# Attention scores with 128-row products, key parts copied to the far halves by DMA, and both masks behind the products

## The chip, the cores and the metric

The program runs on one NeuronCore of a Trainium2 chip. Its engines are named as the profile names them: PE (TensorE, matrix products; PEld is its loading of weights), DVE (VectorE), ACT (ScalarE), POOL (GpSimd) and SP (SyncE). POOL and SP do no arithmetic here, they issue DMAs. The metric is the device time of one execution in microseconds (us).

## What is computed

Two layers over 512 positions of width 2048. Each layer normalises and modulates x, projects it, runs an S5 branch and a differential attention branch, and projects both back. Only the attention's scores are touched in their arithmetic:

```python
def diff_attention(q, k, v, lam, sub_g, lambda_init):
    ...
        sc = jnp.einsum('bqhmd,bkhmd->bhmqk', q_blk, k,
                        preferred_element_type=jnp.float32) * scale
        q_pos = i * Q_BLOCK + jnp.arange(Q_BLOCK)
        mask = key_pos[None, :] <= q_pos[:, None]
        sc = jnp.where(mask, sc, -jnp.inf)
        p = jax.nn.softmax(sc, axis=-1)
        w = p[:, :, 0] - lam * p[:, :, 1]
        return jnp.einsum('bhqk,bkhe->bqhe', w, vf)
```

There are 8 heads of two maps (m = 0, 1), each map with 64 dimensions, and 4 blocks of 128 queries. So scores are made in 2 x 8 x 4 = 64 blocks; block i sees N = 128 (i + 1) keys.

## The kernel before

Every large product is split for accuracy. An operand is held as a high part (rounded to float32r) and a low part (the rest), and one product becomes three: high by high, high by low, low by high (`mm3`). Weights come from memory in units of 128 x 1024 numbers, are split by ACT (`hi`) and DVE (`lo`), and each unit feeds one step of PE work, 24 products of 512 columns in most stages.

The order of instructions is written out in program order by `step`, which emits, between the PE work of one unit and the next, what the generators in `bg` (attention of a head, S5, modulation) have ready. Attention of head h is `attn_gen`. In its round t it emits `scores(t)`, `softmax(t - 1)`, `turn(t - 2)`, `values(t - 3)`, one round for each step. Heads follow each other every six steps, and PE meanwhile goes on with the q, k and gate projections of the next head, or with the GLU.

The two maps lie in the 128 partitions, map 0 in rows 0 to 63 and map 1 in rows 64 to 127. For a map m the tile `qk` holds `qa` (own half: high part of q, far half: low part of q) and `kb` (high part of k in both halves). So one 128-row product of `qa` and `kb` gives high by high plus low by high. The third term, high by low, comes from a product over the 64 rows of the own half of `qa` and of `KL`, the low part of k. Then a bf16 product of the identity and the triangle `maskb` adds the mask. All three write one PSUM bank (`bk5` for map 0, `bk6` for map 1). `qk_split` makes these parts for q (kind 1) and k (kind 0) in a later step than the projection.

Further pieces: `s5_prep` makes the S5 tables, once ahead of each layer, from `are`, `aim` and the step size; `mix` of the S5 output multiplies a tile by a 0/1 pattern `CS_TAP`; at the start the constants `cst` and parameters `par` are loaded ahead of x, and 80 bf16 products (`WARM`) run while x and the first weights arrive. In the first layer's modulation stage, `first_cols` starts a bank with a bf16 product of the identity by a column of zeros spread over 512 columns.

Of the kernel before, what the change touches and what calls it, by code (L numbers as in the profile page):

```python
# [10 lines left out]
F32 = mybir.dt.float32  # L11
F32R = mybir.dt.float32r
BF16 = mybir.dt.bfloat16
I32 = mybir.dt.int32
AF = mybir.ActivationFunctionType
# [6 lines left out]
P = 128  # L22
KT = D // P
NG = 64
# [7 lines left out]
PP_BG = PP_BA + DEPTH * 32  # L32
PP_SG = PP_BG + DEPTH * 16
PP_C = PP_SG + DEPTH
PP_ARE = PP_C + 16
PP_AIM = PP_ARE + DEPTH * NG
PP_W = PP_AIM + DEPTH * NG


CS_ID = 0  # L40
CS_MASK = CS_ID + P
CS_INVF = CS_MASK + P
CS_SG1 = CS_INVF + 1
CS_SG2 = CS_SG1 + 1
CS_SGR = CS_SG2 + 1
CS_TAP = CS_SGR + 1
CS_W = CS_TAP + P


# [3 lines left out]
NR = 2  # L53
NH = 4
SHARED = 8192
SIDE = 2560
WARM = 80


def idle(n):  # L60

    for _ in range(3 * n):
        yield


class Prog:
    def __init__(self, ctx, tc, io):
# [11 lines left out]
        self.lo = [sp.tile([P, 1024], F32R, name=f"lo{i}") for i in range(NH)]  # L79
        self.TOT = 52992 - 2 * KT * S - 2 * NH * 1024 - SHARED - SIDE  # L80
        self.sb = sp.tile([P, self.TOT], F32, name="sb")
# [27 lines left out]
    def v(self, off, n):  # L109
        return self.sb[:, off:off + n]  # L110
# [5 lines left out]
    def side(self, dt, name):  # L116

        self.sd = self.sp.tile([P, SIDE], dt, name=name, tag="side")

    def v2(self, off, n):  # L120
        return self.sd[:, off:off + n]
# [215 lines left out]
def build(ctx, tc, io):  # L337
    q = Prog(ctx, tc, io)
    nc = q.nc
    M, A, SUB = ALU.mult, ALU.add, ALU.subtract  # L340
    v = q.v
# [1 line left out]
    hth, htl = q.hth, q.htl  # L343


    cst = q.alloc(CS_W)
    par = q.alloc(PP_W)
    q.ident = v(cst + CS_ID, P)
    idm = v(q.alloc(128), 128).bitcast(BF16)
    idb, maskb = idm[:, 0:P], idm[:, P:]  # L350
    ones = v(q.alloc(P), P)
    zero = v(q.alloc(2), 2).bitcast(BF16)
    cos_o, sin_o = q.alloc(512), q.alloc(512)
# [12 lines left out]
    v2 = q.v2  # L366

    def pc(col, n=1):
        return v(par + col, n)

    def cc(col, n=1):
        return v(cst + col, n)
# [15 lines left out]
                wt0=(1, 384), wt1=(1, 512), of=(1, 512), sw=(1, 512), sm=(2, 32))  # L388
    ra.p, ra.wt = [ra.p0, ra.p1], [ra.wt0, ra.wt1]

    qa_o, kb_o, kl_o = [0, 512], [1024, 1536], 2048

    s5 = layout(R5, 4416, U=(2, 512), BE=(2, 384), K=(2, 128), D=(2, 128), PR=(1, 512),
                PI=(1, 512), GR=(1, 512), GI=(1, 512), A8=(1, 64))
# [16 lines left out]
    ada_o = [RA, RA + 1024]  # L411


    nc.sync.dma_start(out=v(cst, CS_W), in_=io["cst"])
    nc.sync.dma_start(out=v(par, PP_W), in_=io["par"])
    xt = [q.shared(4 * D, F32, "x0")]
    q.side(F32, "sd0")

    def xv(st, c0=0, n=D):
        return xt[0][:, st * D + c0:st * D + c0 + n]  # L420
# [4 lines left out]
    nc.vector.memset(ones, 1.0)  # L425
    nc.vector.memset(zero, 0.0)
    nc.vector.tensor_copy(out=idb, in_=cc(CS_ID, P))
    nc.vector.tensor_copy(out=maskb, in_=cc(CS_MASK, P))  # L428


    t16 = v(small_o, 16)
# [4 lines left out]
    def setup_gen():  # L436
# [9 lines left out]
        nc.vector.tensor_copy(out=tw[0], in_=posi)  # L446
        q.ts(tw[0], tw[0], cc(CS_INVF), M)
        yield from idle(1)
# [182 lines left out]

    def s5_prep(l):
        T = [v(x, 64) for x in s5.tab]
        are, aim = pc(PP_ARE + NG * l, NG), pc(PP_AIM + NG * l, NG)
        lst, step, xr, th, er, co, si = T[0:7]
        q.dma(lst, io["lstep"][l].partition_broadcast(P))
        yield from idle(3)
        yield from q.exp_acc(step, lst, T[7:10], 64)
        yield from idle(1)
        q.tt(xr, are, step, M)  # L640
        q.tt(th, aim, step, M)
        yield from q.exp_acc(er, xr, T[7:10], 64)
        yield from idle(2)
        yield from q.sincos(co, si, th, T[7:12])
        yield from idle(2)
        PR, PI, GR, GI, TW = (tab3(x) for x in (s5.PR, s5.PI, s5.GR, s5.GI, s5.tw))
        a1r, a1i, nr, den, fr, fi, t0 = T[12:19]
        q.tt(a1r, er, co, M)
        q.tt(a1i, er, si, M)
        q.ts(nr, a1r, 1.0, SUB)  # L650
        q.tt(den, are, are, M)
        q.tt(t0, aim, aim, M)
        q.tt(den, den, t0, A)
        nc.vector.reciprocal(out=den, in_=den)
        yield from idle(1)
        q.tt(fr, nr, are, M)
        q.tt(t0, a1i, aim, M)
        q.tt(fr, fr, t0, A)
        q.tt(fr, fr, den, M)
        q.tt(fi, a1i, are, M)  # L660
        q.tt(t0, nr, aim, M)
        q.tt(fi, fi, t0, SUB)
        q.tt(fi, fi, den, M)
        yield from idle(1)
        nc.vector.tensor_copy(out=PR[:, :, 0], in_=a1r)
        nc.vector.tensor_copy(out=PI[:, :, 0], in_=a1i)
        for n in (1, 2, 4):
            ar = PR[:, :, n - 1].unsqueeze(2).to_broadcast([P, NG, n])
            ai = PI[:, :, n - 1].unsqueeze(2).to_broadcast([P, NG, n])
            yield from q.cmul(PR[:, :, n:2 * n], PI[:, :, n:2 * n], ar, ai, PR[:, :, 0:n], PI[:, :, 0:n], TW[:, :, 0:n])  # L670
            yield from idle(1)
        nc.vector.tensor_copy(out=GR[:, :, 0], in_=fr)
        nc.vector.tensor_copy(out=GI[:, :, 0], in_=fi)
        frb = fr.unsqueeze(2).to_broadcast([P, NG, 7])
        fib = fi.unsqueeze(2).to_broadcast([P, NG, 7])
        yield from q.cmul(GR[:, :, 1:8], GI[:, :, 1:8], frb, fib, PR[:, :, 0:7], PI[:, :, 0:7], TW[:, :, 0:7])
        q.ts(v(s5.GI, 512), v(s5.GI, 512), cc(CS_SG2), M)

        q.ts(v(s5.A8, 64), PI[:, :, 7], cc(CS_SG2), M)
        yield from idle(1)  # L680
# [82 lines left out]
    def s5_state_gen(l):  # L763
# [107 lines left out]
        for j in range(8):  # L871
            if j < 7:
                s5_load_be(l, j + 1, 128)
                load_m(j + 1)
                s5_load_u(l, j + 1)
            be = v(s5.BE[j % 2], 384).rearrange("p (f g q) -> p f g q", f=3, g=8)
            O = o.A[j % 2]
            On4 = O.rearrange("p (g s e) -> p g s e", g=8, s=8)
            T4 = o.T.rearrange("p (g s e) -> p g s e", g=8, s=8)
            pr = PR[:, 8 * j:8 * j + 8, :].unsqueeze(3).to_broadcast([P, 8, 8, 16])  # L880
            pi = PI[:, 8 * j:8 * j + 8, :].unsqueeze(3).to_broadcast([P, 8, 8, 16])
            q.tt(On4, pr, be[:, 1].unsqueeze(2).to_broadcast([P, 8, 8, 16]), M)
            q.tt(T4, pi, be[:, 2].unsqueeze(2).to_broadcast([P, 8, 8, 16]), M)
            q.tt(O, O, o.T, SUB)
            Mb = o.B[j % 2].rearrange("p (g f) -> p g f", g=8)
            q.tt(Mb, Mb, cc(CS_TAP, P).unsqueeze(1).to_broadcast([P, 8, P]), M)
            yield
            if j > 0:
                gelu(j - 1)
            yield  # L890
            b = bank[3 - j % 2]
            U = v(s5.U[j % 2], 512)
            for g in range(8):
                q.mm(b[:, g * 64:(g + 1) * 64], Mb[:, g], U[:, g * 64:(g + 1) * 64], True, False)
                q.mm(b[:, g * 64:(g + 1) * 64], O[:, g * P:(g + 1) * P], X[:, 8 * j + g, 0:64], False, True)
            yield
# [8 lines left out]
    def attn_gen(l, h):  # L905
        n = h % 2
        V, Z = v(ra.v, 512), v(ra.za[n], 512)
        KL = v2(kl_o, 512)
        OF = v(ra.of, 512)
        sm = ra.sm[n]  # L910
        ssum, ssq = v(sm, 8), v(sm + 8, 4)
# [6 lines left out]
        def scores(i):  # L918
            N = (i + 1) * P
            assert S5[l].r == 8  # L920
            for m in range(2):
                qa, r = v2(qa_o[m] + i * P, P), slice(64 * m, 64 * m + 64)
                q.mm(q.sc[m][:, 0:N], qa, v2(kb_o[m], N), True, False)
                q.mm(q.sc[m][:, 0:N], qa[r], KL[r, 0:N], False, False)
                q.mm(q.sc[m][:, i * P:N], idb, maskb, False, True)

        def softmax(i):
# [234 lines left out]
    def layer(l):  # L1162
# [131 lines left out]
        def qk_split(kind):  # L1294
            x = v(ra.x[kind], 512)
            for m in range(2):
                r, far = slice(64 * m, 64 * m + 64), slice(64 - 64 * m, 128 - 64 * m)
                if kind == 0:
                    kb = v2(kb_o[m], 512)
                    q.act(kb[r], x[r], AF.Copy)  # L1300
                    q.act(kb[far], x[r], AF.Copy)
                    q.tt(v2(kl_o, 512)[r], x[r], kb[r].bitcast(F32), SUB)
                else:
                    qa = v2(qa_o[m], 512)
                    q.act(qa[r], x[r], AF.Copy)
                    q.tt(qa[far], x[r], qa[r].bitcast(F32), SUB)
# [259 lines left out]
def _layout(x, c, positions, norm_g, w_ada, b_ada, w_in, w_out, ssm_a_re, ssm_a_im, ssm_b_re, ssm_b_im,  # L1566
# [80 lines left out]
    par[:, PP_SG:PP_C] = pk(sub_g)  # L1647
    par[:, PP_C:PP_ARE] = pk(c)
    par[0:64, PP_ARE:PP_AIM] = ssm_a_re.reshape(-1, 64).T
    par[64:, PP_ARE:PP_AIM] = ssm_a_re.reshape(-1, 64).T  # L1650
    par[0:64, PP_AIM:PP_W] = ssm_a_im.reshape(-1, 64).T
# [4 lines left out]
    cst[:, CS_ID:CS_ID + P] = np.eye(P)  # L1656
    cst[:, CS_MASK:CS_MASK + P] = np.where(r[None, :] <= r[:, None], 0.0, NEG)
    invf = np.float32(10000.0) ** (-np.arange(32, dtype=f) / np.float32(32))
    cst[:, CS_INVF] = invf[r % 32]
    cst[:, CS_SG1] = np.where(r < 64, 1.0, -1.0)  # L1660
    cst[:, CS_SG2] = np.where(r < 64, -1.0, 1.0)
    cst[:, CS_TAP:] = (r[None, :] // 16 + r[:, None] % 8) >= 7
    cst[:, CS_SGR] = np.where(r % 64 < 32, -1.0, 1.0)
# [27 lines left out]
```

## Time and profile before

| | |
|---|---|
| device time, median of 3 runs | 1971.81 us (1969.84 to 1972.72) |
| the profiled execution | 1970.02 us, of which the span from the first to the last instruction is 1967.6 us |
| busy share of the span | PE 99%, PEld 84%, DVE 70%, ACT 41%, POOL 9% |
| the 16 attention heads | about 43 us each, at 441 to 780 us and at 1390 to 1730 us |

The profiled execution's own time is its span and 2.4 us around it, and it lies 1.8 us under the median. Matrix products are pipelined: a product's row in the trace overlaps the next one's, so what a product costs is read from the distance between the starts of two rows, not from the length of a row.

### The profile page before, as it was taken

To read this page: it belongs to the slowest core of one execution; us is meant where nothing else is said; L and a number is where in the kernel's file an instruction comes from. 1 tells how busy PE (TensorE), PEld (TensorE's weight loads), DVE (VectorE), ACT (ScalarE), POOL (GpSimd) and SP (SyncE) were. 2 spreads that over 40 slices of the span, in tenths; PEclk is the share of its full clock that TensorE was granted. 3 is DMA by queue.
4 is the path that set the end of the run, shared out by engine and by line. 5 is a ranking of instruction groups with operands and counts; after the bars stand their busy time and mean duration, and the time that the engine had idled before them with its cause. 6 is when DMAs were issued, how large, how long until landed. Compare 5 with 4: busy or idle time off the path is not lost.

```text
span 1967.6 us, 28067 instructions
## 1 busy us (share of the span) xinstructions
PE 1945.2 (99%) x10552; PEld 1655.1 (84%) x10560; DVE 1371.1 (70%) x2603; ACT 811.7 (41%) x1510; POOL 180.7 (9%) x280
## 2 busy tenths in 40 slices
PE   8999999999999999999999999999999999999998
PEld 7888898888777778888899899888777777888887
DVE  7867866987778787779867434797777776643444
ACT  6333234444444554322245234433444445532222
POOL 0003230220000000000001220032000000000000
PEclk9999999999999999999999999999999999999999
DMA  8976652666555845687544433376655584345323
GB/s 320 367 290 228 193 147 96 207 188 209 157 159 179 198 153 174 223 301 238 169 161 134 127 116 109 99 226 202 184 169 167 156 187 125 97 152 215 97 86 118
DMA packets 117864, 350.38 MB, mean 178 GB/s; under 512 B 31680, under 2 KB 32128, under 8 KB 115296
## 3 DMA queue, kind: packets, MB, share of 16 engines
q1 hardware_dynamic: 97632, 277.27, 44.2%
q0 software_dynamic: 20096, 71.32, 11.6%
q8 instruction: 82, 1.34, 0.3%
q14 instruction: 54, 0.44, 0.1%
HBM read 309.60 MB, written 30.54 MB: 173 GB/s over the span
## 4 chain that ended last, share of the span: by engine, by line
PE 93%; DMA 2%; DVE 2%; issue 1%; ACT 1%; SPq 0%; POOL 0%; ACTq 0%; DVEq 0%
PE bk L143 92%; PE bk L151 2%; DMA sb<-in_wada 2%; DVE lo L128 1%; DMA sb<-in_ssm_d 1%; DVE sb L137 1%; DVE sb L128 0%; DMA sb<-in_w 0%; DVE htl L128 0%; ACT hi L125 0%; ACT sd L125 0%; ACT x L125 0%; DVE sb L132 0%; SPq L424 0%; DVE x L128 0%
## 5 line engine op out<-in xcount | busy, mean ns | idle before, releaser
L128 DVE TENSOR_TENSOR lo<-sb,hi 128x1024 fp32r<-128x1024 f32 x288 | 351.5, 1222 | 404.7 <-ACT hi L125 382.7
L125 ACT ACTIVATE hi<-sb 128x1024 fp32r<-128x1024 f32 x288 | 304.4, 1059 | 624.2 <-PE bk L143 465.4
L143 PE MATMUL bk<-hth,hi 128*128 128x512 f32 x1280 | 512.9, 401 | 0.0
L143 PE MATMUL bk<-hth,lo 128*128 128x512 f32 x1280 | 499.6, 390 | 0.0
L143 PE MATMUL bk<-htl,hi 128*128 128x512 f32 x1280 | 498.8, 390 | 0.0
L143 PE MATMUL bk<-hi,hth 128*128 128x256 f32 (+1 forms) x1088 | 358.1, 329 | 1.7 <-ACT hth L125 1.3
L143 PE MATMUL bk<-hi,htl 128*128 128x256 f32 (+1 forms) x1088 | 355.8, 327 | 0.9 <-DVE htl L128 0.9
L143 PE MATMUL bk<-lo,hth 128*128 128x256 f32 (+1 forms) x1088 | 355.7, 327 | 0.5 <-DVE lo L128 0.5
L137 DVE SCALAR_TENSOR_TENSOR sb<-sb 128x512 f32<-128x512 f32 (+7 forms) x654 | 320.5, 499 | 20.3 <-DMA sb<-in_wada 1.5
L143 PEld LDWEIGHTS bk<-hth,lo 128*128 128x128 f32 x1280 | 240.3, 188 | 51.6
L143 PEld LDWEIGHTS bk<-htl,hi 128*128 128x128 f32 x1280 | 240.9, 188 | 48.1 <-issue 1.9
L143 PEld LDWEIGHTS bk<-hth,hi 128*128 128x128 f32 x1280 | 241.1, 188 | 47.6 <-issue 1.9
L128 DVE TENSOR_TENSOR sb<-sb 128x4 f32<-128x4 f32 (+7 forms) x461 | 220.2, 495 | 22.5 <-DMA sb<-in_ssm_d 8.9
L143 PEld LDWEIGHTS bk<-hi,hth 128*128 128x128 f32 x1088 | 207.0, 190 | 19.8 <-ACT hth L125 1.5
L143 PEld LDWEIGHTS bk<-hi,htl 128*128 128x128 f32 x1088 | 206.9, 190 | 19.0 <-DVE htl L128 1.4
L143 PEld LDWEIGHTS bk<-lo,hth 128*128 128x128 f32 x1088 | 207.0, 190 | 18.0 <-DVE lo L128 0.7
L143 PE MATMUL bk<-sb 128*128 128x128 f32 (+4 forms) x1112 | 165.0, 279 | 7.8 <-DVE sb L428 3.7
L143 PE MATMUL bk<-gt,hi 128*128 128x512 f32 x512 | 159.6, 393 | 0.0
L143 PEld LDWEIGHTS bk<-sb 128*128 128x128 f32 x904 | 118.5, 193 | 9.6 <-issue 3.8
L125 ACT ACTIVATE sb<-bk,sb 128x512 f32<-128x512 f32 (+3 forms) x144 | 77.1, 540 | 104.8 <-DVE sb L132 104.8
L125 ACT ACTIVATE sb<-bk 128x512 f32<-128x512 f32 (+3 forms) x212 | 87.2, 444 | 64.7 <-PE bk L143 34.9
L143 PEld LDWEIGHTS bk<-gt,hi 128*128 128x128 f32 x512 | 94.8, 188 | 18.8
(112 smaller groups left out, 1812.7 us busy)
## 6 DMA issues: line engine op xcount, KB each, us to landing
sb<-in_w SPq DMA_DIRECT2D x288, 512.0 KB, 4.0
sb<-in_wada SPq DMA_DIRECT2D x185, 512.0 KB, 4.7
sb<-uD POOLq DMA_DIRECT2D x32, 256.0 KB, 5.6
ss<-kD POOLq DMA_DIRECT2D x16, 512.0 KB, 6.0
sb<-sb SPq DMA_DIRECT2D x128, 64.0 KB, 3.9
sb<-in_be POOLq DMA_DIRECT2D x32, 192.0 KB, 4.4
x<-in_x SPq DMA_DIRECT2D x4, 1024.0 KB, 11.6
uD<-sd POOLq DMA_DIRECT2D x16, 256.0 KB, 3.2
```

The costliest lines, as they stand in the source:

```text
L125: self.nc.scalar.activation(out=out, in_=in_, func=func, **kw)
L128: self.nc.vector.tensor_tensor(out=out, in0=a, in1=b, op=op)
L137: self.nc.vector.scalar_tensor_tensor(out=out, in0=a, scalar=s, in1=b, op0=op0, op1=op1)
L143: return self.nc.tensor.matmul(out, lhsT=l, rhs=r, start=a, stop=z)
L151: return self.nc.tensor.transpose(out, in_, self.ident)
```

## The change

The product over 64 rows becomes one over 128 rows. For that the low part of k must stand in both halves, so each map gets its own `kl` next to its `kb` in the `qk` tile. `qk_split` computes own halves only (one ACT and one DVE operation for a map), and a DMA from the POOL queue copies `kb` and `kl` of the own half, 64 x 1024 numbers (256 KB), into the far half. The mask products of both maps follow the four score products.

The `qk` tile grows by 512 columns. Room for it is made elsewhere: `CS_MASK` and `CS_TAP` are loaded into the side tile and kept as bf16 only, and `are` and `aim` are no longer resident but are loaded by two POOL DMAs in `s5_prep`.

```diff
-    qa_o, kb_o, kl_o = [0, 512], [1024, 1536], 2048
+    qa_o, kb_o, kl_o = [0, 512], [1024, 2048], [1536, 2560]
...
-    nc.sync.dma_start(out=v(cst, CS_W), in_=io["cst"])
-    nc.sync.dma_start(out=v(par, PP_W), in_=io["par"])
...
+    nc.sync.dma_start(out=v(cst, CS_P), in_=io["cst"][:, 0:CS_P])
+    nc.sync.dma_start(out=v2(2560, 2 * P), in_=io["cst"][:, CS_P:CS_W])
+    nc.sync.dma_start(out=v(par, PP_P), in_=io["par"][:, 0:PP_P])
...
-    nc.vector.tensor_copy(out=maskb, in_=cc(CS_MASK, P))
+    nc.vector.tensor_copy(out=maskb, in_=v2(2560, P))
+    nc.vector.tensor_copy(out=tapb, in_=v2(2560 + P, P))
...
-        are, aim = pc(PP_ARE + NG * l, NG), pc(PP_AIM + NG * l, NG)
+        are, aim = T[19:21]
+        q.dma(are, io["par"][:, PP_ARE + NG * l:PP_ARE + NG * (l + 1)])
+        q.dma(aim, io["par"][:, PP_AIM + NG * l:PP_AIM + NG * (l + 1)])
...
-            q.tt(Mb, Mb, cc(CS_TAP, P).unsqueeze(1).to_broadcast([P, 8, P]), M)
+            q.tt(Mb, Mb, tapb.unsqueeze(1).to_broadcast([P, 8, P]), M)
...
             for m in range(2):
-                qa, r = v2(qa_o[m] + i * P, P), slice(64 * m, 64 * m + 64)
+                qa = v2(qa_o[m] + i * P, P)
                 q.mm(q.sc[m][:, 0:N], qa, v2(kb_o[m], N), True, False)
-                q.mm(q.sc[m][:, 0:N], qa[r], KL[r, 0:N], False, False)
+                q.mm(q.sc[m][:, 0:N], qa, v2(kl_o[m], N), False, False)
+            for m in range(2):
                 q.mm(q.sc[m][:, i * P:N], idb, maskb, False, True)
...
-                    kb = v2(kb_o[m], 512)
+                    kb, kl = v2(kb_o[m], 512), v2(kl_o[m], 512)
                     q.act(kb[r], x[r], AF.Copy)
-                    q.act(kb[far], x[r], AF.Copy)
-                    q.tt(v2(kl_o, 512)[r], x[r], kb[r].bitcast(F32), SUB)
+                    q.tt(kl[r], x[r], kb[r].bitcast(F32), SUB)
+                    both = v2(kb_o[m], 1024)
+                    q.dma(both[far], both[r])
```

On PE, the last score block of a head (i = 3, N = 512, here head 0 of layer 0) stands as follows, before and then after. `bk5_81` and `bk6_82` are the score banks of the two maps, `qk0` the tile of q and k parts, `sb_75` as an operand of the 128x128 products behind a LDWEIGHTS row is identity and mask, and the row ahead is the last product of a projection.

```order
L143 MATMUL bk1_77<-hth_65,lo1_72 128x512
L143 MATMUL bk5_81<-qk0_2990 128x512 x2
L143 LDWEIGHTS sb_75
L143 MATMUL bk5_81<-sb_75 128x128
L143 MATMUL bk6_82<-qk0_2990 128x512 x2
L143 LDWEIGHTS sb_75
L143 MATMUL bk6_82<-sb_75 128x128
L143 MATMUL bk2_78<-sb_75 128x128
```

```order
L145 MATMUL bk1_77<-hth_65,lo1_72 128x512
L145 MATMUL bk5_81<-qk0_2994 128x512 x2
L145 MATMUL bk6_82<-qk0_2994 128x512 x2
L145 LDWEIGHTS sb_75
L145 MATMUL bk5_81<-sb_75 128x128
L145 LDWEIGHTS sb_75
L145 MATMUL bk6_82<-sb_75 128x128
L145 MATMUL bk2_78<-sb_75 128x128
```

Each "x2" is the product with `kb` and the one with the low part of k; before, the second of them is the one over 64 rows, now both are over 128. The mask of map 0 moved from between the maps to behind them.

On the POOL queue the two copies of a head stand where that head's k is split. This is the place of head 0 of layer 0, before and after; `uD0`, `yD0` and `vD0` are tensors in memory (S5 input, S5 output, values), `ss0` the S5 tile.

```order
L140 DMA ss0_1217<-kD0_88 128x8x128
L140 DMA sb_75<-uD0_84 128x8x64
L140 DMA yD0_86<-sb_75 128x8x64 x2
L140 DMA sb_75<-vD0_90 128x4x128
L140 DMA yD0_86<-sb_75 128x8x64
```

```order
L142 DMA ss0_1221<-kD0_88 128x8x128
L142 DMA sb_75<-uD0_84 128x8x64
L142 DMA qk0_2994<-qk0_2994 64x1024 x2
L142 DMA yD0_86<-sb_75 128x8x64 x2
L142 DMA sb_75<-vD0_90 128x4x128
L142 DMA yD0_86<-sb_75 128x8x64
```

The copies stand ahead of the stores of the S5 output that DVE and ACT finish later; nothing else on this queue moved.

## Rows read from the trace of the kernel before

**Rows 1.** The page's chain that ended last: share of the span by engine.

```profile
PE 93%; DMA 2%; DVE 2%; issue 1%; ACT 1%; SPq 0%; POOL 0%; ACTq 0%; DVEq 0%
```

**Rows 2.** PE's waits, whole span, longest first: us in total, times, longest.

```profile
PE bk L143 <- DVE sb L428: 3.7, 1, 3.7
...
```

**Rows 3.** Busy time in windows over the 16 heads: sum and mean.

```profile
...
sum 675.00, PE 675.00 PEld 536.40 DVE 502.46 ACT 338.76 POOL 25.67; mean PE 42.19 PEld 33.53 DVE 31.40 ACT 21.17 POOL 1.60
```

**Rows 4.** PE timeline, score block N = 512: start us, us, engine, line, operation.

```profile
507.56 0.39 PE L143 MATMUL bk<-hth,lo 128*128 128x512 f32 x1
507.79 0.82 PE L143 MATMUL bk<-qk 128*128 128x512 f32 x2
...
508.11 0.50 PE L143 MATMUL bk<-qk 64*128 64x512 f32 x1
...
508.54 0.23 PE L143 MATMUL bk<-sb 128*128 128x128 bf16 x1
508.57 0.90 PE L143 MATMUL bk<-qk 128*128 128x512 f32 x2
509.41 0.51 PE L143 MATMUL bk<-sb 128*128 128x128 bf16 x3
```

**Rows 5.** Weight loads of the same block; in brackets the idle time before.

```profile
507.56 0.19 PEld L143 LDWEIGHTS bk<-qk 128*128 128x128 f32 x1
508.10 0.18 PEld L143 LDWEIGHTS bk<-qk 64*128 64x128 f32 x1 [0.35 <-issue]
508.53 0.10 PEld L143 LDWEIGHTS <-sb 128*128 128x128 bf16 x1 [0.24 <-issue]
```

**Rows 6.** PE timeline, blocks of 128, 256 and 384 keys of the same head.

```profile
486.33 0.83 PE L143 MATMUL bk<-sb 128*128 128x128 f32 x6
486.92 0.56 PE L143 MATMUL bk<-qk 128*128 128x128 f32 x2
...
487.94 0.23 PE L143 MATMUL bk<-sb 128*128 128x128 bf16 x1
...
493.53 0.59 PE L143 MATMUL bk<-qk 128*128 128x256 f32 x2
...
494.70 0.23 PE L143 MATMUL bk<-sb 128*128 128x128 bf16 x1
...
500.65 0.79 PE L143 MATMUL bk<-qk 128*128 128x384 f32 x2
...
502.13 0.23 PE L143 MATMUL bk<-sb 128*128 128x128 bf16 x1
```

**Rows 7.** PE timeline in the first modulation stage, around the zero product of `first_cols`.

```profile
57.06 0.40 PE L143 MATMUL bk<-hth,lo 128*128 128x512 f32 x1
57.52 0.61 PE L143 MATMUL bk<-sb 128*128 128x128 f32 x4
```

**Rows 8.** Weight load of that zero product.

```profile
57.29 0.10 PEld L143 LDWEIGHTS <-sb 128*128 128x128 bf16 x1 [0.27 <-issue]
```

**Rows 9.** Timelines, head 6 of layer 0: its k subtractions, its first scores.

```profile
689.33 1.38 DVE L128 TENSOR_TENSOR qk<-sb,qk 64x512 fp32r<-64x512 f32 x2
...
700.29 0.56 PE L143 MATMUL bk<-qk 128*128 128x128 f32 x2
```

**Rows 10.** DMA issues by line: KB each, median us to landing.

```profile
sb<-uD POOLq DMA_DIRECT2D x32, 256.0 KB, 5.6
```

**Rows 11.** Timeline of the start: parameter loads, and DVE's wait for x.

```profile
1.19 0.42 SPq L415 DMA_DIRECT2D sb<-in_par  x1
1.25 0.67 POOL L140 DMA_DIRECT2D sb<-in_lstep  x1 [0.81 <-POOLq L1679]
...
19.74 0.17 DVE L134 TENSOR_SCALAR sb<-sb 128x4 f32<-128x4 f32 x1 [2.32 <-ACT hth L125]
```

**Rows 12.** DVE groups by shape, 370 to 442 us (S5 output, layer 0): busy, mean ns.

```profile
L128 DVE TENSOR_TENSOR ss<-ss,sb 128x1024 f32<-128x1024 f32 x12 | 14.4, 1221 | 0.8 <-DMA ss<-kD 0.7
```

**Rows 13.** Busy time in 15 windows of 9 us of that stage, both layers.

```profile
...
sum 135.00, PE 135.00 PEld 120.48 DVE 111.84 ACT 51.16 POOL 40.66; mean PE 9.00 PEld 8.03 DVE 7.46 ACT 3.41 POOL 2.71
```

More of the change, by code (lines that the diff above doesn't have):

```diff
@@ L34 @@
 PP_C = PP_SG + DEPTH
-PP_ARE = PP_C + 16
+PP_P = PP_C + 16
+PP_ARE = PP_P
 PP_AIM = PP_ARE + DEPTH * NG
@@ L40 @@
 CS_ID = 0
-CS_MASK = CS_ID + P
-CS_INVF = CS_MASK + P
+CS_INVF = CS_ID + P
 CS_SG1 = CS_INVF + 1
@@ L45 @@
 CS_SGR = CS_SG2 + 1
-CS_TAP = CS_SGR + 1
+CS_P = CS_SGR + 1
+CS_MASK = CS_P
+CS_TAP = CS_MASK + P
 CS_W = CS_TAP + P
@@ L55 @@
 SHARED = 8192
-SIDE = 2560
+SIDE = 3072
 WARM = 80
@@ L343, in build @@
     hth, htl = q.hth, q.htl
-    cst = q.alloc(CS_W)
-    par = q.alloc(PP_W)
+    cst = q.alloc(CS_P)
+    par = q.alloc(PP_P)
     q.ident = v(cst + CS_ID, P)
-    idm = v(q.alloc(128), 128).bitcast(BF16)
-    idb, maskb = idm[:, 0:P], idm[:, P:]
+    idm = v(q.alloc(192), 192).bitcast(BF16)
+    idb, maskb, tapb = idm[:, 0:P], idm[:, P:2 * P], idm[:, 2 * P:]
+    idm = idm[:, 0:2 * P]
     ones = v(q.alloc(P), P)
@@ L907, in attn_gen @@
         V, Z = v(ra.v, 512), v(ra.za[n], 512)
-        KL = v2(kl_o, 512)
         OF = v(ra.of, 512)
```

## The prediction

> **What bounds the kernel now.** I read the chain of waits first: PE holds 93% of it [rows 1], so a change that shortens PE's work shortens the program wherever PE never waits. The view of waits shows how rarely it does: no wait of it adds up to more than 3.7 us in the whole span, and the longest is at the start [rows 2]. Then the stages. In the windows over the sixteen heads PE is busy for all of its 42.19 us a window, DVE for 31.40, ACT for 21.17 [rows 3]. So a microsecond that PE saves in a head is a microsecond of the program, until another engine fills the head. The heads also hold the only place where PE does something odd, and the timeline of PE and of its weight loads shows it.
>
> **What a score block costs before.** I measure from the start of its first product to the start of its second mask; what follows the second mask is the same before and after. With 512 keys: 507.79 to 509.41, 1.62 us [rows 4]. The products alone, at the distance of ordinary 512-column products (507.56 to 507.79, 0.227 us), would be 4 x 0.227 = 0.91. The rest is in the steps into and out of the 64-row product. The 128-row product at 507.79 is followed 0.32 us later by the 64-row one at 508.11, which is followed 0.43 us later by the mask at 508.54: 0.09 and 0.20 too much [rows 4]. The weight loads say why. A load for 128 rows starts with the product ahead of it (507.56, both views) and is hidden under it; the 64-row load starts at 508.10, with its own product, after PE's loading side stood idle 0.35 us, and the mask's load again waits, to 508.53, behind the 64-row product [rows 4, 5]. So PE runs empty on the way into 64 rows and on the way back. The other blocks cost 486.92 to 487.94 (1.02), 493.53 to 494.70 (1.17) and 500.65 to 502.13 (1.48) [rows 6].
>
> **What it costs afterwards.** Four 128-row products, of which the last is followed by a bf16 load, and one mask ahead of the second mask.
> - Products: 0.227 us for 512 columns [rows 4]. For 128 columns the distance of the 128-column products ahead of the smallest block: 0.111 (six of them take 0.83 us from 486.33, and the first score product at 486.92 stands 0.03 behind the start of the last) [rows 6]. Between these, 384 and 256 columns take at least their proportion of 512 (0.170 and 0.114) and at most the straight line from 0.111 to 0.227 (0.188 and 0.150).
> - The step from a 128-row product of the large kind to a bf16 product: the program before has it, in the first modulation stage. There a product at 57.06 is followed by an unrecorded bf16 product of 512 columns, whose load stands at 57.29, and the next product starts at 57.52: 0.46 us for two times 512 columns, 0.23 each [rows 7, 8]. The load does come late, but nothing is lost, so I put this step at 0. The other end is the 0.20 above.
> - First mask to second mask: no two bf16 products of 128 columns stand together in the trace. Below: 128 columns in proportion to 512, 0.057. Above: 0.111, the distance of 128-column products with full loads [rows 6]. I take 0.08.
> - Where short products precede the block, its first product is recorded 0.08 early (486.92 is those 0.03 behind the last of the six, not 0.111) and its distance to the next is longer by as much [rows 6]. That holds for the blocks of 128 and 384 keys, before and after, so 0.08 is added there.
>
> Blocks then cost 0.91 + 0.08 = 0.99 (512 keys), 0.08 + 0.44 + 0.08 = 0.60 (128), and at the lower distances 0.08 + 0.68 + 0.08 = 0.84 (384) and 0.46 + 0.08 = 0.54 (256). Saved: 0.63, 0.42, 0.64 and 0.63, together 2.32 us a head; at the upper distances the last two save 0.57 and 0.48, together 2.10. I take 2.25, nearer the proportion, since a product of 256 columns has twice the columns under which a load is hidden at 0.111. Times 16: **36.0 us**, bounds 33.6 and 37.1.
>
> **A rule against it.** The Trainium skill, "TensorE: Matmul & The Clock Gate", Part 3 on packing small matmuls, says that a weight load overlaps a running product only when the row groups differ. By that, four products on the same 128 rows would each pay their load, and the change would lose time; that is the fourth rival below. This case's trace disagrees: the load at 507.56 runs beside a product on the same rows [rows 4, 5]. Another page of the Trainium skill, "TensorEngine Tiling (Array Packing)", section "Tiling Modes", under key properties, says that changing the tiling mode drains the engine while changing the tile does not; by that rule nothing drains in the new block, which bears out the 0 above, and the trace agrees for the way into and out of 64 rows.
>
> **The rest of the change.**
> - ACT loses 32 copies of a half. ACT is busy half of a head [rows 3], so this is worth nothing by itself; it lets the subtractions come a little earlier.
> - POOL gains 32 copies of 256 KB. Cost nothing, hidden by the time between k's split and the first scores. The tightest head that I found is head 6: the second subtraction ends at 690.71, the first score product starts at 700.29, 9.6 us later [rows 9]. The nearest DMA in size on that queue lands in 5.6 us [rows 10]; with two issues of 0.67, as of another DMA on that queue [rows 11], that is 6.9, a margin of 2.7 us. Without that cover every head would wait. Queued behind the copies on POOL are the load of v, wanted three steps later, and in head 0 the stores of the S5 output, which wait for DVE until after the copies anyway.
> - The first product of each map in `scores(0)` now waits for a copy as well as for DVE. If the copy has landed this costs nothing.
> - The start: one more SP issue ahead of the loads of x, 0.42 us, and x and the weights behind it gate the first products: **+0.4 us**. On POOL the step size is issued two DMAs later, 2 x 0.67 = 1.3 us; DVE's table work ahead of the norm shifts with it, but DVE stood idle 2.32 us there [rows 11]. Bounds 0 to 1.7 us.
> - `mix`'s multiplication now reads bf16 in one operand: 16 operations of 1.22 us [rows 12]. I take no change; if the mixed operand doubled it, DVE has 9.00 - 7.46 = 1.5 us idle in the 9 us of each [rows 13]. Before layer 1, `are` and `aim` are loaded by two small DMAs with nothing waiting.
>
> **Sum.** 1970.0 (the profiled execution's own time) - 36.0 + 0.4 = 1934.4. It lies 1.8 us under the median of the runs shown, so as a median **1936 us**. Its own range: the product distances move it by -1.1 to +2.4 us, the mask's by up to 64 x 0.03 = 2 either way, the start by -0.4 to +1.3, the median by about 1.5: 1932 to 1941.
>
> **Rivals.**
> 1. *The bf16 load still empties PE.* Then 0.20 us of the old block stays in each of the 64: 12.8 us back, **1949**. For it: the masks' loads are late in the old block, and the zero product's load is late too [rows 5, 8]. Against: no time is lost around the zero product [rows 7].
> 2. *Another engine fills the head.* DVE would have to find its 31.4 us in 40.0; on average it does, but its work is uneven, and PE could begin to wait on `lo` or on the softmax. Half a microsecond to one a head gives back 8 to 16 us: **1944 to 1952**. Against: PE waits nowhere in the heads now [rows 3].
> 3. *The copies come late* (slower). If a copy takes 11 us instead of 5.6, the first scores wait 11 + 1.3 - 9.6 = 2.7 us in each head, 43 us in all: **1979**. Priced with the tightest head; it decides from about 10.5 us of landing on, where the wait eats 2.25 us a head. Against: the stage moves little data on POOL, and 5.6 us is the median of 32 like-sized DMAs [rows 10].
> 4. *Loads are not hidden on equal rows* (slower): 256 score products pay 0.19 each [rows 5], 49 us; less the 36 saved, **1985**. The trace speaks plainly against it.
> 5. *The 64 rows are not what costs*, but the second product into a bank; the 128-row product then pays the same: **1972**. Against: projections send 24 products into one bank at 0.227 us each.
>
> **How the numbers follow.** Chances: forecast 0.78, first rival 0.10, second 0.05, third 0.03, fourth 0.02, fifth 0.02. The forecast's own range leaves 0.22 outside, so I widen it over the first rival: 1932 to 1949. A measurement of this kernel can tell about 0.2% (4 us) from no change. Faster: forecast, first and second rival, 0.93; within 0.2%: the fifth, 0.02; slower: the third and fourth, 0.05.
>
> **What would show it.** Right: in the 512 block four products 0.23 us apart, no idle before their loads, the mask's load late but the first mask 0.23 to 0.24 us behind the fourth product, heads of about 40.9 us instead of 43, no PE wait for a DMA in the heads. Wrong: a distance of 0.4 us ahead of the first mask (first rival), PE waiting for `qk` copies (third) or for `lo` (second), or a first product later than 20 us into the span (start).

## The result: 1939.3 us instead of 1972.2

| | before | changed |
|---|---|---|
| device time, median of 4 runs | 1972.20 us (1969.84 to 1972.72) | 1939.32 us (1938.70 to 1940.49) |
| ratio | | 0.9836, 95% interval 0.9819 to 0.9853 |
| the profiled execution, its span | 1970.02 us, 1967.6 us | 1940.49 us, 1938.7 us |

The change wins 32.9 us between the medians and 29.5 between the two profiled executions. 1936 was forecast, with a range of 1932 to 1949.

**The block.** PE's timeline of the changed kernel, score block N = 512 of the head of [rows 4], in five narrow stretches, so that each product's start shows (a row ends with the last product that it counts):

```profile
504.24 0.62 PE L145 MATMUL bk<-qk 128*128 128x512 f32 x2
504.47 0.61 PE L145 MATMUL bk<-qk 128*128 128x512 f32 x2
504.70 0.61 PE L145 MATMUL bk<-qk 128*128 128x512 f32 x2
504.92 0.39 PE L145 MATMUL bk<-qk 128*128 128x512 f32 x1
505.15 0.28 PE L145 MATMUL bk<-sb 128*128 128x128 bf16 x2
```

The weight loads of the same block:

```profile
504.02 0.87 PEld L145 LDWEIGHTS bk<-qk 128*128 128x128 f32 x4
505.15 0.12 PEld L145 LDWEIGHTS <-sb 128*128 128x128 bf16 x2 [0.26 <-issue]
```

The four products start 0.22 to 0.23 us apart, the distance of the ordinary 512-column products in [rows 4]. Their loads begin at 504.02, one product ahead, with no idle between them. The mask's load is late, as foretold, and nothing is lost: the first mask starts 0.23 behind the fourth product. Before, 0.32 and 0.43 stood between these products [rows 4].

Blocks of 128 and 256 keys, the same head:

```profile
485.12 0.64 PE L145 MATMUL bk<-qk 128*128 128x128 f32 x4
485.60 0.28 PE L145 MATMUL bk<-sb 128*128 128x128 bf16 x2
...
491.26 0.63 PE L145 MATMUL bk<-qk 128*128 128x256 f32 x4
491.74 0.29 PE L145 MATMUL bk<-sb 128*128 128x128 bf16 x2
```

To the first mask it is 0.48 us in both. Counted from a block's first product to the product after its second mask, a typical block (the median of the 16 heads) went from 1.06 to 0.58 us (128 keys), 1.20 to 0.57 (256), 1.54 to 0.93 (384) and 1.69 to 1.03 (512). That saves 0.48, 0.63, 0.62 and 0.65 us, 2.39 us a head before rounding. The same saving is seen in whole heads. The next view has the first seven heads of layer 0, in windows that run from the first score block of one head to that of the next, before and then changed (the windows of [rows 3] are of other lengths, so their mean of 42.19 us is not the length of a head):

```profile
sum 301.61, PE 301.61 PEld 240.18 DVE 227.72 ACT 153.78 POOL 12.02; mean PE 43.09 PEld 34.31 DVE 32.53 ACT 21.97 POOL 1.72
```

```profile
sum 284.90, PE 284.90 PEld 238.20 DVE 227.62 ACT 144.82 POOL 19.75; mean PE 40.70 PEld 34.03 DVE 32.52 ACT 20.69 POOL 2.82
```

**What was given back.** 16 x 2.39 is 38.2 us, and the span became only 28.9 shorter. The chain that ended last has less PE than in [rows 1]. In the view of PE's waits the first two of the following lines stood before as well, with 3.7 us each at the most [rows 2]; the wait for q's split (`qk`) is new, and the one for ACT's `sb` had been 0.4 us:

```profile
PE 89%; DVE 4%; DMA 3%; issue 1%; ACT 1%; SPq 0%; POOL 0%; ACTq 0%; DVEq 0%
```

```profile
PE bk L145 <- DMA sb<-in_wada: 4.5, 1, 4.5
PE bk L145 <- DVE sb L433: 3.6, 1, 3.6
PE bk L145 <- DVE qk L130: 2.5, 1, 2.5
PE bk L145 <- ACT sb L127: 1.9, 5, 0.6
```

I compared the distance from each score block to the next in both traces. It is shorter by the same amounts everywhere but for four places. The start gives back 0.6 us (first score block at 442.3 instead of 441.7). Head 8, the first of layer 1 counted from 0, gives back 5.8 in the distances to and from its first block. Head 13 gives back 2.4, and the step to the last block of head 7 0.5. Together that is 9.3, and 38.2 less 9.3 is 28.9.

**Head 8.** The changed kernel's queues and DVE there, SP first, then POOL, then DVE:

```profile
1359.48 3.62 SPq L1354 DMA_DIRECT2D sb<-sb  x4
```

```profile
1359.91 0.54 POOL L142 DMA_DIRECT2D qk<-qk  x1 [3.41 <-DVE qk L130]
1360.63 0.52 POOL L142 DMA_DIRECT2D qk<-qk  x1 [0.18 <-issue]
1361.15 0.80 POOL L142 DMA_DIRECT2D sb<-vD  x1
```

```profile
1369.01 2.02 DVE L130 TENSOR_TENSOR sb<-sb 128x512 f32<-128x512 f32 x3 [8.67 <-DMA sb<-sb]
```

The four small DMAs at 1359.48 are `qk_out`'s swaps of q, which `rope` needs. The two copies of k, 512 KB, go out beside them, and DVE waits 8.67 us for the swaps. Before, that wait was 5.6 us:

```profile
DVE sb L128 <- DMA sb<-sb: 5.6, 1, 5.6
```

So q is split about 3 us late, and PE, which before met this split just in time, stands still. What follows is in PE's timeline and in one window:

```profile
1375.70 1.41 PE L145 MATMUL bk<-qk 128*128 128x128 f32 x4 [2.48 <-DVE qk L130]
...
1378.53 0.63 PE L145 MATMUL bk<-hth,hi 128*128 128x512 f32 x1
1378.96 0.63 PE L145 MATMUL bk<-htl,hi 128*128 128x512 f32 x1
```

```profile
1375.00:1380.00 5.00, 4.27 (x13) 3.51 (x14) 4.90 (x7) 1.06 (x1) 0.00 (x0) 0.53 0.88 277
```

The wait itself is 2.48 us. Behind it the granted clock of the window is 0.53, so 1.2 GHz for nearly all of it, and 512-column products stand 0.43 us apart instead of 0.227. The slow clock costs 3.0 us, about as much again as the wait: by so much is the distance from this block to the next longer than the other heads' saving would have it.

**Head 13.** PE waits twice there, and both times it is a score product that waits for the softmax of the block before, which still reads the score bank. ACT's exponentials of that softmax in turn waited for DVE. PE first, then ACT:

```profile
1593.85 1.07 PE L145 MATMUL bk<-qk 128*128 128x384 f32 x4 [0.61 <-ACT sb L127]
```

```profile
1593.23 0.47 ACT L127 ACTIVATE sb<-bk,sb 128x256 f32<-128x256 f32 x1 [1.73 <-DVE sb L134]
```

### The profile page after: what moved, and what is told of

It reads as the page before. It is cut to its first block, busy times and chain, and to the rows that moved or that the text cites. A ratio compares the mean times of both kernels' runs of the same rounds, so it can differ in the third digit from the quotient of the medians.

```text
span 1938.7 us, 28170 instructions
## 1 busy us (share of the span) xinstructions
PE 1911.3 (99%) x10552; PEld 1652.2 (85%) x10560; DVE 1371.1 (71%) x2604; ACT 790.7 (41%) x1478; POOL 200.5 (10%) x316
## 4 chain that ended last, share of the span: by engine, by line
PE 89%; DVE 4%; DMA 3%; issue 1%; ACT 1%; SPq 0%; POOL 0%; ACTq 0%; DVEq 0%
PE bk L145 88%; PE bk L153 2%; DVE lo L130 1%; DMA sb<-in_wada 1%; DVE sb L139 1%; DMA sb<-in_w 1%; DMA sb<-in_ssm_d 1%; DVE sb L130 1%; DMA sb<-sb 1%; ACT hi L127 0%; DMA sb<-yD 0%; DVE sb L134 0%; DVE sb L939 0%; ACT sb L127 0%; SPq L1354 0%
## 5 line engine op out<-in xcount | busy, mean ns | idle before, releaser
L145 PE MATMUL bk<-sb 128*128 128x128 f32 (+4 forms) x1112 | 153.6, 278 | 8.6 <-DMA sb<-in_wada 4.5
```

The lines of the kernel that those rows point to most:

```text
L145: return self.nc.tensor.matmul(out, lhsT=l, rhs=r, start=a, stop=z)
```

## The experiments

Each kernel ran beside the kernel before on the same chip, but not all on one chip; the ratios are to the time of the kernel before there. In the diffs, "changed" is the kernel of the prediction.

**1. The masks between the maps again** (changed, one line less: the masks back in the loop of the products).

```diff
                 q.mm(q.sc[m][:, 0:N], qa, v2(kl_o[m], N), False, False)
-            for m in range(2):
                 q.mm(q.sc[m][:, i * P:N], idb, maskb, False, True)
```

> The changed kernel, with each map's mask again right behind its two products (all four score products stay over 128 rows). My theory (it is the steps between 128 and 64 rows that cost): a block gets one bf16-to-fp32r step more and no step of rows, so at most 0.05 us for each of the 64 blocks, 0 to 3 us over the changed kernel: 1939 to 1942 us. Rival (the bf16 mask between the maps is what cost, and the move of the masks is the gain): at least half of the 33 us comes back, 1955 to 1972 us.

1941.35 us, ratio 0.985 (0.9835 to 0.9864). All 64 blocks together, counted as above, take 54.1 us instead of 51.1: 0.05 us a block, as my theory said. PE's timeline, the block of 512 keys:

```profile
502.88 0.61 PE L145 MATMUL bk<-qk 128*128 128x512 f32 x2
503.33 0.23 PE L145 MATMUL bk<-sb 128*128 128x128 bf16 x1
503.37 0.71 PE L145 MATMUL bk<-qk 128*128 128x512 f32 x2
503.93 0.51 PE L145 MATMUL bk<-sb 128*128 128x128 bf16 x3
```

The order of the masks is worth some 3 us at the most, not 33.

**2. The masks alone moved** (kernel before).

```diff
                 q.mm(q.sc[m][:, 0:N], qa[r], KL[r, 0:N], False, False)
+            for m in range(2):
                 q.mm(q.sc[m][:, i * P:N], idb, maskb, False, True)
```

> The kernel before, with only the masks moved behind the four products; the low product stays over 64 rows and nothing is copied by DMA. My theory: two steps into 64 rows and two out of them remain in each block, so 1969 to 1975 us, as before. Rival (the masks' place is the gain): half of the 33 us or more is won, 1939 to 1956 us.

1972.45 us, ratio 1.0008 (0.9999 to 1.0018). As my theory said, and the rival is out: the gain isn't the masks' place.

**3. Half the dose** (changed; map 1's low product over rows 64 to 127 again).

```diff
-                q.mm(q.sc[m][:, 0:N], qa, v2(kl_o[m], N), False, False)
+                r = slice(64 * m if m else 0, 128)
+                q.mm(q.sc[m][:, 0:N], qa[r], v2(kl_o[m], N)[r], False, False)
```

> The changed kernel, with the low product of map 1 again over 64 rows (rows 64 to 127); map 0 and everything else as changed. My theory: one pair of steps (into 64 rows and out of it) remains of two, about half of the gain is given back: 1954 to 1958 us, a block of N = 512 near 1.34 us. Rival (masks or the DMA copies decide): 1939 to 1942 us.

1954.5 us, ratio 0.9918 (0.9903 to 0.9932): half the gain is gone. In PE's timeline of the block, again in narrow stretches, the three 128-row products stand 0.23 apart, and the 64-row one 0.32 behind the third; the mask follows it after 0.42 (507.76):

```profile
506.56 0.62 PE L145 MATMUL bk<-qk 128*128 128x512 f32 x2
506.79 0.61 PE L145 MATMUL bk<-qk 128*128 128x512 f32 x2
507.02 0.81 PE L145 MATMUL bk<-qk 128*128 128x512 f32 x2
507.34 0.49 PE L145 MATMUL bk<-qk 64*128 64x512 f32 x1
```

**4. Both 64-row products next to each other** (kernel before, no copies by DMA).

```diff
+            qa = [v2(qa_o[m] + i * P, P) for m in range(2)]
+            for m in range(2):
+                q.mm(q.sc[m][:, 0:N], qa[m], v2(kb_o[m], N), True, False)
+            for m in range(2):
+                r = slice(64 * m, 64 * m + 64)
+                q.mm(q.sc[m][:, 0:N], qa[m][r], KL[r, 0:N], False, False)
             for m in range(2):
-                qa, r = v2(qa_o[m] + i * P, P), slice(64 * m, 64 * m + 64)
-                q.mm(q.sc[m][:, 0:N], qa, v2(kb_o[m], N), True, False)
-                q.mm(q.sc[m][:, 0:N], qa[r], KL[r, 0:N], False, False)
                 q.mm(q.sc[m][:, i * P:N], idb, maskb, False, True)
```

> The kernel before, with a block's products in the order 128 rows map 0, 128 rows map 1, 64 rows map 0 (rows 0 to 63), 64 rows map 1 (rows 64 to 127), mask, mask; no DMA copies. My theory prices a step between 128 and 64 rows whichever way: two steps a block instead of four, about half of the 33 us, 1954 to 1958 us. If the step from rows 0-63 to rows 64-127 empties the engine as well, three of four remain, about 1964 us. If the two 64-row products run side by side, one of them costs nothing: 0.21, 0.16, 0.11 and 0.05 us less in a block of N = 512 to 128, 8.5 us over 16 heads, about 1947 us, and more where the loads of the two also fall together. Rival (it is the masks' place): as with the masks alone moved.

1942.35 us, ratio 0.9857 (0.984 to 0.9873), better than any of the three figures; it is the third case, with the loads falling together as well. PE's timeline of the block, in a narrow stretch, and the weight loads:

```profile
505.13 0.50 PE L143 MATMUL bk<-qk 64*128 64x512 f32 x2
505.57 0.23 PE L143 MATMUL bk<-sb 128*128 128x128 bf16 x1
```

```profile
504.37 0.41 PEld L143 LDWEIGHTS bk<-qk 128*128 128x128 f32 x2
505.13 0.19 PEld L143 LDWEIGHTS bk<-qk 64*128 64x128 f32 x2 [0.35 <-issue]
505.56 0.11 PEld L143 LDWEIGHTS <-sb 128*128 128x128 bf16 x2 [0.24 <-issue]
```

From the start of the two 64-row products to the mask it is 0.44 us, and with one alone it was 0.43 [rows 4]; both loads together take 0.19. The two row halves work side by side. One pair of steps is left (0.35 and 0.24 us of idle on the loading side), and a typical block is only 0.07 to 0.17 us longer than the changed one. That different tiles of the array load weights and multiply in parallel is what the Trainium skill says ("TensorEngine Tiling (Array Packing)", "Tiling Modes", key properties); the trace agrees, with 0.44 us for two products and 0.43 for one.

**5. The far halves by ACT and DVE** (changed, no copies in any head).

```diff
                     q.act(kb[r], x[r], AF.Copy)
+                    q.act(kb[far], x[r], AF.Copy)
                     q.tt(kl[r], x[r], kb[r].bitcast(F32), SUB)
-                    both = v2(kb_o[m], 1024)
-                    q.dma(both[far], both[r])
+                    q.tt(kl[far], x[r], kb[r].bitcast(F32), SUB)
```

> The changed kernel, with the far halves of kb and kl written by one more ACT and one more DVE operation for a map instead of by the 32 POOL copies of 256 KB. Theory (in head 8, the first of layer 1, the copies fall together with the four swaps of q, which DVE still waits for 8.7 us after the last operation that it could do; q's split is late, PE stands 2.5 us and then runs 6.8 us at half clock): that place comes back to its usual pace, 5 to 6 us less, 1933 to 1936 us; no PE wait on the split at about 1376 us and no stretch below full clock there. Rival (the loss there comes from PE reaching the place earlier, whatever makes the copies): 1938 to 1941 us, with the wait and the half clock as they are. Second rival (ACT and DVE in their place are late elsewhere): above 1941 us. The slower pace in head 13 is left out of the theory: the kernel with paired 64-row products has it too and has no copies, so it should stay.

1939.7 us, ratio 0.9845 (0.983 to 0.9859): no gain in the time, although head 8 is back at its usual pace (PE waits 0.3 us there, no half clock). The second rival's mechanism came true as well, though the time stayed under its 1941 us: around head 6 2.6 us are now given back and in head 13 3.0, and PE's small waits on ACT add up to 3.7 us instead of 1.9:

```profile
PE bk L145 <- ACT sb L127: 3.7, 9, 0.9
```

**6. The far halves by ACT and DVE in head 8 alone.**

```diff
-                    both = v2(kb_o[m], 1024)
-                    q.dma(both[far], both[r])
+                    if (l, h) == (1, 0):
+                        q.act(kb[far], x[r], AF.Copy)
+                        q.tt(kl[far], x[r], kb[r].bitcast(F32), SUB)
+                    else:
+                        both = v2(kb_o[m], 1024)
+                        q.dma(both[far], both[r])
```

> The changed kernel, with the far halves of one head alone (the first of layer 1, head 8 when the 16 are counted from 0) written by ACT and DVE; the other 15 heads keep the copies by DMA. Theory (the copies of this one head, beside q's swaps, are what costs there): nearly the whole 5 to 6 us that all engine copies give, 1933 to 1936 us. Rival (the copies cost a little in every head): a sixteenth of what all engine copies give, 1939 us.

1934.62 us (1934.39 to 1935.84), ratio 0.982 (0.9805 to 0.9835). DVE's wait for the swaps and PE's wait for the split in that stretch:

```profile
DVE sb L130 <- DMA sb<-sb: 4.7, 1, 4.7
```

```profile
PE bk L145 <- DVE qk L130: 0.3, 1, 0.3
```

The granted clock behind that split is 1.00 in this variant:

```profile
1372.00:1377.00 5.00, 4.72 (x24) 3.67 (x23) 4.87 (x8) 1.06 (x1) 0.00 (x0) 1.00 0.84 268
```

Around head 8 the distances between score blocks give back 0.5 us instead of 5.8, so that head's copies cost 5.3 us, as the theory asked. In the time it shows less sharply: 4.7 us between the medians, which were not taken side by side, and 3 by the ratios, whose intervals overlap; on one chip with it, experiment 10, which keeps all the copies, lies 5.7 us above.

**7. The changed kernel again, and a variant that turned out to be it** (the copies of head 8 put off by one step).

```diff
+                    if (l, h) == (1, 0):
+                        q.later(1, lambda far=far, r=r, both=both: q.dma(both[far], both[r]))
+                    else:
+                        q.dma(both[far], both[r])
-                    q.dma(both[far], both[r])
```

> The changed kernel itself once more, beside the three variants that run with it, so that they are compared on one chip: 1937 to 1941 us, PE waiting 2 to 3 us on q's split at about 1375 us in the trace.

> The changed kernel; the two POOL copies of head 8 (the first of layer 1, counted from 0) go out one step later, about 9 us, behind that head's V load and, by the trace, behind q's swaps. Theory (what costs in head 8 is that copies and V load share the DMA engines with q's swaps): the swaps come as early as with that head's copies made by the engines, DVE's wait for them falls from 8.7 us to about 4.7, no PE wait at 1375 us, no half clock there, 4 to 5 us less than the changed kernel. Rival (copies of that head cost wherever they stand, or come too late for the first score now): the same time as the changed kernel or more, PE waiting at the first score.

1938.68 us (0.983, 0.9817 to 0.9844) and 1939.66 us (0.9837, 0.9824 to 0.9851). Nothing else stood on POOL's queue between the two places, so the edit moved no DMA: the copies still went out at 1360.43, ahead of the V load. It tells nothing on the theory, and counts as a further run of the changed kernel: DVE's wait is 8.4 and 8.8 us in the two.

**8. The V load of head 8 ahead of its copies.**

```diff
+            if kind == 0 and (l, h) == (1, 0):
+                q.dma(v(ra.v, 512).rearrange("p (j e) -> p j e", j=4),
+                      q.vD[l][:, h * P:(h + 1) * P].rearrange("(j p) e -> p j e", p=P))
...
-            if t == 1:
+            if t == 1 and (l, h) != (1, 0):
```

> The changed kernel; on the POOL queue the V load of head 8 (the first of layer 1, counted from 0) stands ahead of that head's two copies instead of behind them. The copies still go out when k's split is done, beside q's swaps; the V load goes out about 5 us earlier. Theory 1 (what holds q's swaps up is that the V load, queued behind the waiting copies, falls on them too): DVE's wait for the swaps falls from 8.4 to 8.8 us to 5 or 6, PE's wait on q's split from 2.2 to 2.6 us to under 0.5, and 3 to 5 us are won, 1934 to 1937 us. Theory 2 (the 512 KB of the copies alone hold them up): the waits and the time of the changed kernel, 1938 to 1941 us.

1939.25 us, ratio 0.9836 (0.9823 to 0.985). The V load goes out at 1357.21 now instead of 1361.15, and the swaps are hardly earlier:

```profile
DVE sb L130 <- DMA sb<-sb: 7.9, 1, 7.9
```

PE waits 1.7 us for the split and then runs at half clock again. So nearly all of it comes with the two copies themselves (theory 2); the V load's place is worth 0.5 to 0.9 us of DVE's wait.

**9. The GLU's work a step later** (changed; in `glu_gen`).

```diff
             for j in range(4):
                 load(j)
-            yield from idle(1)
+            yield from idle(2)
```

> The changed kernel; the GLU's ACT and DVE work begins two steps after its first loads instead of one. Theory (in head 13 ACT stands 5.9 us on the first of these loads, in front of the probabilities that PE turns next; PE, which is faster now, reaches these 1.3 us too early in sum and five small waits follow): ACT's wait goes, PE's waits on ACT there with it, 1.5 to 2.5 us less than the changed kernel. Rival (the small waits come from ACT's load of work in these heads, not from that wait): no difference, or a little more time, since the GLU ends later.

1938.36 us, ratio 0.9833 (0.9819 to 0.9846). ACT's wait for `yD` is gone from the trace of that stretch, PE's waits on ACT are not:

```profile
PE bk L145 <- ACT sb L127: 1.2, 2, 0.9
```

My theory of head 13 falls. It also had the wrong work in mind: as shown above, the waiting products are scores, and they wait for the softmax, not for the turned probabilities.

**10. More products at the start** (changed, `WARM = 110` instead of 80).

> The changed kernel with 110 instead of 80 bf16 products at the start. Theory (PE's 4.5 us without work ahead of the first modulation product are followed by 6.83 us at the half clock, 3.41 us of it more than in the kernel before, and these 3.41 us cost half of themselves): 30 products at about 0.11 us end 3.2 us later, the wait falls to about 1.3 us, the half-clock stretch goes or falls to 3.4 us: 1.5 to 3.5 us less, 1936 to 1938 us. Rival (the products that start there wait for weights anyway, so the clock costs nothing there): no change, 1939 to 1940 us.

1940.34 us (1938.32 to 1941.67), ratio 0.985 (0.9834 to 0.9867). The changed kernel's start in two windows, and PE's first modulation product in the variant:

```profile
18.00:22.00 4.00, 3.53 (x16) 3.56 (x17) 3.38 (x21) 1.52 (x3) 0.00 (x0) 0.50 1.03 411
22.00:26.00 4.00, 4.00 (x31) 4.00 (x30) 3.48 (x18) 3.46 (x2) 0.00 (x0) 0.79 1.03 405
```

```profile
20.40 1.80 PE L145 MATMUL bk<-sb 128*128 128x128 f32 x14 [1.70 <-DVE sb L130]
```

The half clock at the start (0.50 and 0.79) goes; the variant's trace has 1.00 in both windows. But now PE waits for DVE and begins with them at 20.40 instead of 18.47. The profiled execution reaches the first score block 1.6 us earlier, but that is no evidence: with the start of the changed kernel unaltered, the traces of the experiments reach it anywhere from 440.5 to 443.1, and this one did at 440.7. The median of four shows nothing. From the first modulation product to the first score block those traces took 421.9 and 422.0 us where the half clock lasted 3.4 us, and 422.9 to 424.7 where it lasted 6.8; the variants with 110 products, with none of it, took 420.3 and 420.8. The kernel before had 422.6 with 3.4 us of it, and its two variants (2, 4) 422.5 and 422.4 with 6.8. So what the half clock there costs in the time stays open.

**11. Three edits together**: those of 6, 9 and 10.

```diff
+                    if (l, h) == (1, 0):
+                        q.act(kb[far], x[r], AF.Copy)
+                        q.tt(kl[far], x[r], kb[r].bitcast(F32), SUB)
...
-            yield from idle(1)
+            yield from idle(2)
...
-WARM = 80
+WARM = 110
```

> The changed kernel with three edits together: far halves of head 8 by ACT and DVE, GLU work a step later, 110 products at the start. If the losses add: 4.7 us of head 8, 2 of head 13 and 1 to 2 of the start under the changed kernel, 1930 to 1932 us. If the start is worth nothing in the median, as with that edit alone, and head 13 stays: 1934 us.

1934.83 us (1932.36 to 1935.14), ratio 0.9811 (0.9798 to 0.9824), beside 1935.55 to 1939.3 of the changed kernel on the same chip. It is no better than experiment 6. Head 8 is not free here although it has no copies: DVE waits 6.0 us for the swaps, PE 1.2 for the split, and PE's next 3 us windows have clocks of 0.88 and 0.55:

```profile
1371.60:1374.60 3.00, 2.52 (x12) 2.12 (x13) 2.94 (x5) 1.06 (x1) 0.00 (x0) 0.88 0.83 303
1374.60:1377.60 3.00, 3.00 (x9) 2.29 (x9) 2.83 (x6) 0.06 (x1) 0.00 (x0) 0.55 0.71 253
```

There the 1 MB load that POOL had issued ahead of the swaps (`in_bgate`) took 8.5 us to land, against 6.4 in experiment 6, so other traffic than the copies seems to hold the swaps up as well. The runs line up: a swap wait of 4.7 us costs PE 0.3, of 6.0 1.2, of 7.9 1.7, of 8.7 2.5.

## Why the prediction was right

- **The steps between 128 and 64 rows are the gain**: shown. Half the steps give half the gain (3), the masks' order gives none of it without them (2) and 3 us with them (1), and one pair of steps with the 64-row products side by side costs 0.07 to 0.17 us a block (4). The block of 512 keys adds up: 1.03 us changed, 1.12 with a mask between the maps (1), 1.32 with one 64-row product (3). One mask between (0.08) and two visits to 64 rows (0.29 each) on top of 1.03 make the 1.69 of before.
- **Blocks saved, 36.0 us**: mis-sized by little, 2.39 us a head measured for 2.25 taken (2.35 in the forecast's own measure, which ends at the second mask), 38.2 for 36.0, and above the upper bound of 37.1. The block of 128 keys saved more than forecast, 0.47 us for 0.42, and the 2.25 was put under the 2.32 of the lower distances, near which the products came out. The products of 256 keys stood 0.12 us apart, near the proportion; mask to mask took 0.066 (0.08 taken); the step to the mask cost nothing, as taken, so the first rival is out.
- **The start, +0.4**: 0.6 measured, which the runs can't tell from 0.4 or from nothing, since traces with the same start differ by up to 2.5 us at the first score block (10). The mechanism isn't confirmed either: the first modulation product was earlier than before (18.47 against 19.09), not later, and then the clock was at half for longer, 0.50 and 0.79 in the windows above, 0.71 and 0.86 before.
- **`mix` with its bf16 operand**: nothing, as taken. The operations of [rows 12] took 1220 ns each, 1221 before, and DVE is busy for 35.2 us of the 40 from 395 to 435 us in both traces.
- **The POOL copies, nothing**: the step that failed, for one head. The cover that I named held: no first score waited for a copy, and the copies landed in 4.0 us (median; 2.8 to 7.5), under the 5.6 taken. But I looked only at who needs the copies and at the queue behind them, not at who shares the DMA engines with them. In head 8 those are q's swaps, whose reader had no slack: 5.3 of the 5.8 us lost there go with that head's copies (6, 8). That the copies hold the swaps up by sharing the DMA engines is argued; that they hold them up is shown. That DMAs run on the same 16 engines and interleave, whichever engine started them, is what the Trainium skill says ("DMA: Bandwidth & Descriptors", "Issuing engines are not separate DMA queues"), and the trace agrees: SP's swaps were held up by POOL's copies, 8.4 to 8.8 us of wait against 4.7.
- **Another engine fills the head** (second rival, 8 to 16 us): in small, 2.9 us in heads 7 and 13, where PE waits on the softmax, as that rival said. It comes with each kernel that has most of the gain, with or without the copies (4, 5, 6), and neither with half of it nor with the masks alone (2, 3). That PE comes too early for the softmax there is argued; in head 13 ACT's exponentials themselves stood 1.73 us for DVE, so ACT was not overloaded just then. Why it is these heads stays open since 9 failed.

The sum forecast 1934.4 us for a profiled execution, and 1940.5 was measured, 6.1 more. It took 2.2 us too little for the blocks, and it lacked 8.9 us of loss (9.3 less the 0.4 for the start), most of them in head 8. That makes 6.7; the time around the span became 0.6 shorter (2.4 before, 1.8 changed), which leaves the 6.1. Between the medians the miss is only 3.3: the forecast added 1.8 to come from the profiled execution to the median, and the changed kernel's profiled execution lies 1.2 over its median. So the mechanism was right, and that the median came so near is in part luck, an underestimated gain and a scatter that covered an unforeseen loss.

## What to carry to other kernels

Price a product that leaves half of the rows idle by the distances to its neighbours, not by its own length: here a visit to 64 rows cost 0.29 us on top at 512 columns (0.40 where two came one right behind the other, experiment 2), more than a full 512-column product, so filling it to 128 rows and pairing it with one on the other half both paid. Where copies move from an engine to DMA, don't only ask whether they land in time: look which small transfers fly at that moment and how much slack their readers have, in every head, and in the first of a layer above all. Here fifteen heads carried the copies for nothing, and one lost 5 us by them.

## What was not expected of the hardware

- The step out of 64 rows cost 0.19 to 0.20 us at 256 to 512 keys and 0.14 at 128, whether a mask came next or a 128-row product (experiment 2). The step into them cost 0.09 behind ordinary products (map 0 before, experiments 3 and 4), but 0.19 to 0.20 at 256 to 512 keys where the 128-row product ahead had itself just come out of 64 rows (experiment 2). That is why moving the masks alone won nothing. Map 1 of the kernel before looks alike, with 0.41 us between its two products, but its first product stands behind a mask, and there even two 128-row products stand 0.32 apart (experiment 1): the step is 0.09 again.
- Two 64-row products on opposite halves, each with its load, took the time of one (0.44 us to the mask, 0.43 with one).
- A PE wait of 2.48 us was followed by a stretch at half clock that cost about as much again (products 0.43 us apart instead of 0.227), and one of 1.2 us by such a stretch as well (experiment 11, 0.55 in a window). One of 0.3 us was followed by none (experiment 6), and neither was the 1.2 us wait at 1012 us between the layers (1.00 from 1010 to 1020 us in the changed kernel's trace). So the length of the last wait alone doesn't tell.
